# A two-layer hybrid decoder trunk on one core: the bytes at which the matmul operands start in SBUF are moved

## The chip, the cores and the metric

The program runs on one core of one Trainium2 chip. The metric is device time in microseconds (us) of one execution. The engines are named as in the profile: PE (TensorE matmul), PEld (TensorE weight load, which overlaps PE), DVE (VectorE), ACT (ScalarE), POOL (GpSimd), SP (SyncE, which here only issues DMAs). SBUF is the on-chip working memory of 128 partitions, PSUM the accumulators that the matmuls write. "Address" below always means the byte at which a buffer starts within each partition of SBUF.

## The reference, cut to what matters

```python
D_MODEL, SEQ, DEPTH = 2048, 256, 2            # one batch, float32 everywhere
def reference(x, ...):
    for l in range(DEPTH):
        h = rms_norm(x, norm_w[l])
        u = h @ w_in[l]                       # 2048 x 7692, cut into 12 parts
        y_conv = conformer_conv(...) * silu(c_gate)    # GLU, depthwise conv of 31, LayerNorm, 512x512 matmul
        y_gdn  = gated_deltanet(...)                   # 6 heads, chunked delta rule
        y_att  = dilated_attention(...) * silu(a_gate) # 12 heads, three strided windows
        x = x + concatenate([y_conv, y_gdn, y_att]) @ w_out[l]   # 2048 x 2048
    return rms_norm(x, final_norm_w)
```

The two large products, by `w_in` and `w_out`, are most of the arithmetic.

## The kernel before

**Precision by three products.** The matmuls of L448 and L457 take float32r operands. To keep float32 accuracy, every operand is held as a high part and a low part: the normalised activations in `HT[0]`, `HT[1]`, the branch outputs in `YT[0]`, `YT[1]`, and each block of weights, after its DMA into a `raw` buffer, as `whi` (ACT, L188) and `wlo = raw - whi` (DVE, L196). A product is then three matmuls: high by high, low by high, high by low.

**The two forms of a product.** `unit` (L448) makes the matmuls of one k-block (128 rows of the product's inner dimension). Where the result is wanted with channels on the partitions (`chan`), 128 columns of `whi` or `wlo` are loaded as stationary weights and 256 columns of `HT[..][:, k, :]` stream past: 18 or 24 matmuls for a k-block pair of a 384- or 512-wide block, each of 256 columns. Otherwise 128 columns of `HT` or `YT` are the stationary operand and the 384 (or 396, 512, 256) columns of `whi` or `wlo` stream. Every matmul has a weight load of 128 columns of its own, and the load for the next matmul runs while the present one streams. `last_unit` (L457) does the last block of the last layer, whose split weights are kept in `HT`: there 128 columns of `YT` are stationary and 256 columns of `HT` stream, 96 matmuls in all.

```python
if chan:
    o = acc[t // 2][:, (t % 2) * S:(t % 2 + 1) * S]
    terms = [(hi[:, a, s], A[0][:, k, :]), (hi[:, a, s], A[1][:, k, :]), (lo[:, a, s], A[0][:, k, :])]
else:
    o = acc[t][:, :n]
    terms = [(A[0][:, k, s], hi[:, a, :n]), (A[1][:, k, s], hi[:, a, :n]), (A[0][:, k, s], lo[:, a, :n])]
```

**The order of the work.** A small planner (`Plan`) runs generators as tasks against guessed costs and thereby writes one fixed order of instructions for each engine. The projections run back to back; between their matmuls stand the small float32 matmuls (`mms`, L229) and transposes (`trs`, L236) of the three branches. A layer takes its jobs in this order: scalars and gates, the delta-rule and convolution inputs (mostly `chan`), the attention inputs (not `chan`), the remaining gates (`chan`), then `w_out` in blocks of 384 and 512 (not `chan`). The weights come through 4 `raw`, 3 `whi` and 3 `wlo` buffers of 4 KB a partition, used in turn. The planner knows no addresses.

**Where buffers lie.** Tiles are placed in the order in which they are made, pool after pool: `cp` (constants and the operands `HT`, `YT`), `wp` (`raw`, `whi`, `wlo`), `sp` (work buffers `b768`, `b1024` and so on, all called `b` in the profile). The first tile of `cp` starts at byte 16,512, behind 16,384 bytes for DMA descriptors and four constants. A k-block of `HT` or `YT` is 1,024 bytes, a stationary slice of 128 columns 512 bytes, and a `whi` row of 384 columns 1,536 bytes, so within a form all operands stand at one and the same remainder of 512 bytes. (The 396-wide block of each layer is the exception: its second k-block stands 48 bytes further.)

Of the kernel before, what the change touches and what calls it, by code (L numbers as in the profile page):

```python
# [11 lines left out]
F32 = mybir.dt.float32  # L12
# [16 lines left out]
NT = S // 128  # L29
# [9 lines left out]
W_OUT_BLOCKS = [[(384 * i, 384) for i in range(4)] + e for e in ([(1536, 512)], [(1536, 256), (1792, 256)])]  # L39

P_CW, P_DW, P_DB, P_LW, P_LB, P_GN, P_AL, P_DT, PCOLS = 16, 88, 212, 216, 220, 224, 225, 231, 237


class Event:
# [128 lines left out]
def hybrid_trunk(ctx, tc, x, x_t, w_in, conf_pw_w, w_out, params, final_norm_w, rope, lnc, out):  # L173
    nc = tc.nc
    cp = ctx.enter_context(tc.tile_pool(name="consts", bufs=1))
    wp = ctx.enter_context(tc.tile_pool(name="weights", bufs=1))
# [18 lines left out]
    def tt(out_, a, b, op):  # L195
        return ("dve", 70 + _free(out_) / 0.96, lambda: nc.vector.tensor_tensor(out_, a, b, op=op))  # L196

    def ts(out_, a, s1, s2, op0, op1=None):
        extra = 60 if not isinstance(s1, (int, float)) else 0

        def emit():
            if op1 is None:
                nc.vector.tensor_scalar(out_, a, s1, None, op0=op0)  # L203
            else:
                nc.vector.tensor_scalar(out_, a, s1, s2, op0=op0, op1=op1)
        return ("dve", 70 + _free(out_) / 0.96 + extra, emit)
# [44 lines left out]
    def many(n, cols, name, dt=F32, pool=None):  # L251
        return Slots([(pool or sp).tile([128, cols], dt, name=f"{name}{i}", tag=f"{name}{i}") for i in range(n)])

    HT = [cp.tile([128, KB, S], F32R, name=f"HT{i}") for i in range(2)]
    YT = [cp.tile([128, KB, S], F32R, name=f"YT{i}") for i in range(2)]
    RAW = Slots([wp.tile([128, 1024], F32, name=f"raw{i}") for i in range(4)])
    WHI = Slots([wp.tile([128, 1024], F32R, name=f"whi{i}") for i in range(3)])
    WLO = Slots([wp.tile([128, 1024], F32R, name=f"wlo{i}") for i in range(3)])
    S768 = many(14, 768, "b768_")
    S1024 = many(3, 1024, "b1024_")  # L260
    S512 = many(2, 512, "b512_")
# [22 lines left out]
    upper = cp.tile([128, 128], F32, name="upper")  # L284
    lower = cp.tile([128, 128], F32, name="lower")
    lowr = cp.tile([128, 128], F32R, name="lowr")
    lncs = cp.tile([128, 384], F32, name="lncs")
    ropes = cp.tile([128, NT, 32], F32, name="ropes")
    pw_neg = cp.tile([128, HC], F32, name="pw_neg")
    PAR = [cp.tile([128, PCOLS], F32, name=f"par{l}") for l in range(DEPTH)]  # L290
    GNH = [cp.tile([128, 1], F32, name=f"gnh{l}") for l in range(DEPTH)]
# [7 lines left out]
           for l, p in enumerate([X_PIECES] + [PIECES] * (DEPTH - 1) + [LAST_PIECES])]  # L299
    RSTD = [cp.tile([128, NT], F32, name=f"rstd{l}") for l in range(DEPTH + 1)]  # L300
    sums = cp.tile([128, NT], F32, name="sums")
    HALF = [cp.tile([128, NT], F32, name=f"half{l}") for l in range(DEPTH)]
    ROW = [cp.tile([128, S], F32, name=f"row{l}") for l in range(DEPTH)]
    misc_ready = [Event() for _ in range(DEPTH)]
# [31 lines left out]
    def split(hi, lo, src, scale):  # L336

        yield act(hi, src, scale=scale)
        yield stt(lo, src, scale, hi.bitcast(F32), ALU.mult, ALU.subtract)
# [19 lines left out]
    def load_xt(k0, m):  # L359

        buf = yield ("get", S768)
        yield ("dma", 128 * m * S * 4 / 330.0, lambda: nc.sync.dma_start(  # L362
# [3 lines left out]
    def norm_xt(k0, m, buf):  # L366
        yield ("wait", misc_ready[0])
        for b in range(m):
            k = k0 + b
            yield from split(HT[0][:, k, :], HT[1][:, k, :], buf[:, b * S:(b + 1) * S], PAR[0][:, k:k + 1])  # L370
            yield ("set", h_ready[0][k])
        yield ("put", S768, [buf])

    def load_x(j):

        c0, n = X_PIECES[j]
        buf = yield ("get", S768)
        xs = buf[:, :NT * n].rearrange("p (t c) -> p t c", t=NT)
        yield ("dma", 128 * NT * n * 4 / 330.0, lambda: nc.sync.dma_start(
            xs, xf[:, c0:c0 + n].rearrange("(t p) c -> p t c", p=128)))  # L380
        plan.spawn(sums_x(j, xs, buf), 3)
        if j == len(X_PIECES) - 1:
            nc.sync.dma_start(lncs, lnc)
            nc.sync.dma_start(ropes, rope.rearrange("(t p) c -> p t c", p=128))

    def sums_x(j, xs, buf):
        yield from square_sums(0, j, [xs[:, t] for t in range(NT)], nsq0[j])
        yield ("put", S768, [buf])

    def load_weights(order):  # L390
        for i in order:
# [3 lines left out]
            if i in X_BEFORE:  # L395
                yield from load_x(X_BEFORE[i])
            raw = yield ("get", RAW)
            view = raw[:, :m * n].rearrange("p (a n) -> p a n", n=n)
# [8 lines left out]
    def split_weights(order):  # L407
        for i in order:
# [3 lines left out]
            if keep is None:  # L412
                hb = yield ("get", WHI)
                lb = yield ("get", WLO)
                hi, lo = (b[:, :m * n].rearrange("p (a n) -> p a n", n=n) for b in (hb, lb))
                w_ready[i][1] = (hi, lo, hb, lb)
            else:
                hi, lo = (b[:, keep:keep + m, :] for b in HT)
                w_ready[i][1] = (hi, lo, None, None)
# [9 lines left out]
    def split_lo(i, hi, lo, raw, view, e):  # L429
        yield ("wait", e)  # L430
        yield tt(lo, view, hi.bitcast(F32), ALU.subtract)
        yield ("put", RAW, [raw])
        yield ("set", w_ready[i][0])

    def unit(acc, hi, lo, a, n, A, k, first, last, chan):


        def emit():
            for t in range(n // 128 if chan else NT):
                s = slice(t * 128, (t + 1) * 128)  # L440
# [6 lines that stand above are left out]
                for i, (w, m) in enumerate(terms):  # L447
                    nc.tensor.matmul(o, w, m, start=first and i == 0 and not (chan and t % 2), stop=last and i == 2,  # L448
                                     skip_group_check=chan)
        return ("pe", 6 * (n / 2.4 + 2.5), emit)  # L450

    def last_unit(acc, t, k, n):

        def emit():
            s = slice(t * 128, (t + 1) * 128)
            for i, (w, m) in enumerate(((0, 0), (1, 0), (0, 1))):
                nc.tensor.matmul(acc[t][:, :n], YT[w][:, k, s], HT[m][:, k, :n], start=k == 0 and i == 0,  # L457
                                 stop=k == KB - 1 and i == 2)
        return ("pe", 3 * (n / 2.4 + 2.5), emit)

    def project(jobs):
# [15 lines left out]
        for (A, ready, w, c0, n, order, then, prio, before, chan), first in todo:  # L477
# [10 lines left out]
            for i, (k0, m) in enumerate(order):  # L488
                yield ("wait", w_ready[first + i][0])
                hi, lo, hb, lb = w_ready[first + i][1]  # L490
                for a in range(m):
                    k = k0 + a
                    yield ("wait", ready[k])
                    yield unit(acc, hi, lo, a, n, A, k, i + a == 0, i == len(order) - 1 and a == m - 1, chan)
                yield ("put", WHI, [hb])
                yield ("put", WLO, [lb])
            plan.spawn(then(acc), prio)
# [7 lines left out]
    def square_sums(l, j, xs, ev):  # L505
        for t in range(NT):
            yield act(JUNK[:, :_free(xs[t])], xs[t], AF.Square, accum=SSQ[l][:, t, j:j + 1])
        yield ("set", ev)
# [26 lines left out]
    def norm_128(l, k, ps, xs, done):  # L535
        yield trs(*((ps[:, t * 128:(t + 1) * 128], xs[t]) for t in range(NT)))
        yield ("wait", misc_ready[l])
        yield from split(HT[0][:, k, :], HT[1][:, k, :], ps, PAR[l][:, k:k + 1])
        yield ("set", h_ready[l][k])
        yield ("set", done)  # L540

    def finish_norm(l, evs, t0=0, t1=NT):
# [9 lines left out]
        if l == DEPTH:  # L552
            yield ("set", final_ready[t0])
            return
        yield ts(HALF[l], r, 0.125, None, ALU.mult)
        yield ("set", rstd_ready[l])
# [7 lines left out]
    def layer(l):  # L564
        par = PAR[l]
        cw, dw = par[:, P_CW:P_CW + 72], par[:, P_DW:P_DW + 4 * CW]
        rstd, half = RSTD[l], HALF[l]
        y_ready = [Event() for _ in range(KB)]
# [129 lines left out]
        def v3(t):  # L698

            return t.rearrange("p (a b) -> p a b", b=128)  # L700

        def scalars(acc):
            z = yield ("get", S768)
            gd["Z1"] = z.rearrange("p (t c) -> p t c", t=NT)
# [29 lines left out]
        def decay(b):  # L734
            t, i = divmod(b, 2)
            if i == 0:
                gd["EM"][t], gd["L%d" % t] = (v3(b_) for b_ in (yield ("get", S768, 2)))
                yield ("set", gd["E"][t])
# [490 lines left out]
        def inp(c0, n, then, prio, chan=False):  # L1229
            order = full if l or jobs else halved  # L1230
            jobs.append((HT, h_ready[l], win, c0, n, order, then, prio, None, chan))
        inp(GZ + 384, 396, scalars, 6)
# [98 lines left out]
```

## Time and profile before

| | |
|---|---|
| time, 3 runs | median 982.97 us (981.93 to 983.8) |
| the profiled execution's own time | 982.4 us |
| its span, first to last instruction | 980.7 us |
| PE busy | 968.4 us, 99% of the span, 7259 matmuls |
| PEld busy | 946.3 us, 96% |
| DVE busy | 749.3 us, 76% |
| ACT busy | 550.8 us, 56% |
| DMA | 179.01 MB, mean 183 GB/s |
| mean granted TensorE clock | 0.997 of full speed |

The matmuls' ends are modelled by the profiler, and one matmul's duration (some 280 ns for 256 columns) overlaps those of its neighbours; what a matmul costs the stream is the distance from its start to the start of the next. That distance is read here from the chain of work that ended last: where a piece of the chain is nothing but matmuls of one shape, its length divided by their number is the distance.

### The profile page before, as it was taken

What the parts mean: (1) busy time and instruction counts of PE and PEld (TensorE: products, weight loads), DVE (VectorE), ACT (ScalarE), POOL (GpSimd) and SP (SyncE); (2) the same over time, 40 slices, a digit from 0 to 9 for tenths busy, and PEclk for the clock granted to TensorE, in tenths of its full rate; (3) what the DMA queues carried; (4) which work ended last, traced back from release to release, by engine and by line L of the source; (5) the groups of instructions that cost most, each with busy time, mean ns of one, the idle gap of its engine ahead of it and who ended that gap; (6) DMA issues with size and microseconds to landing.
All of it is one profiled execution on the core that took longest, in us unless ns stands there. A gap on an engine that the chain in (4) does not pass through costs nothing.

```text
span 980.7 us, 19060 instructions
## 1 busy us (share of the span) xinstructions
PE 968.4 (99%) x7259; PEld 946.3 (96%) x7259; DVE 749.3 (76%) x1519; ACT 550.8 (56%) x1079; POOL 48.5 (5%) x70
## 2 busy tenths in 40 slices
PE   8999999999999999999999999999999999999996
PEld 7999999999999999999899999999899999999996
DVE  7687799999999666655558768999999976666672
ACT  7764355446685764554455633554466767544551
POOL 1002100200010000000000020002000100000000
PEclk9999999999999999999999999999999999999998
DMA  9765565644445535776655545556344556366672
GB/s 328 254 195 169 175 191 180 186 146 145 146 138 174 178 113 181 224 239 219 214 190 193 192 161 175 186 180 188 128 147 140 155 182 200 127 192 213 220 248 87
DMA packets 67037, 179.01 MB, mean 183 GB/s; under 512 B 8000, under 2 KB 12224, under 8 KB 66944
## 3 DMA queue, kind: packets, MB, share of 16 engines
q1 hardware_dynamic: 64880, 173.85, 54.7%
q0 software_dynamic: 1632, 3.02, 1.2%
q8 instruction: 57, 0.93, 0.4%
q10 hardware_dynamic: 432, 0.91, 0.3%
q14 instruction: 36, 0.29, 0.1%
HBM read 172.77 MB, written 4.98 MB: 181 GB/s over the span
## 4 chain that ended last, share of the span: by engine, by line
PE 97%; DVE 1%; DMA 1%; issue 1%; SPq 0%; ACT 0%; POOLq 0%; POOL 0%; DVEq 0%; ACTq 0%
PE acc L448 87%; PE mix L229 6%; PE mix L236 3%; DMA b<-in_x_t 1%; PE acc L457 1%; PE mix L747 0%; DVE wlo L196 0%; DVE b L193 0%; SPq L404 0%; SPq L362 0%; DVE inv L209 0%; ACT whi L188 0%; POOLq L1327 0%; POOL rstd L245 0%; DVE PTs L203 0%
## 5 line engine op out<-in xcount | busy, mean ns | idle before, releaser
L188 ACT ACTIVATE whi<-raw 128x768 fp32r<-128x768 f32 (+4 forms) x389 | 339.7, 873 | 361.4 <-PE acc L448 320.6
L196 DVE TENSOR_TENSOR wlo<-raw,whi 128x768 fp32r<-128x768 f32 (+4 forms) x389 | 385.5, 991 | 186.4 <-ACT whi L188 182.7
L448 PE MATMUL acc<-HT,whi 128*128 128x256 f32 x2304 | 411.0, 280 | 0.0
L448 PEld LDWEIGHTS acc<-HT,whi 128*128 128x128 f32 x2304 | 351.6, 188 | 1.5 <-issue 1.5
L448 PE MATMUL acc<-HT,wlo 128*128 128x256 f32 x1152 | 321.4, 279 | 0.0
L448 PE MATMUL acc<-whi,HT 128*128 128x384 f32 (+1 forms) x1024 | 271.1, 346 | 0.7 <-ACT whi L188 0.6
L448 PEld LDWEIGHTS acc<-HT,wlo 128*128 128x128 f32 x1152 | 216.0, 188 | 0.0
L448 PEld LDWEIGHTS acc<-whi,HT 128*128 128x128 f32 x1024 | 180.1, 189 | 3.3 <-ACT whi L188 1.4
L448 PE MATMUL acc<-wlo,HT 128*128 128x384 f32 (+1 forms) x512 | 172.9, 338 | 0.8 <-DVE wlo L196 0.8
L448 PE MATMUL acc<-whi,YT 128*128 128x384 f32 (+2 forms) x640 | 163.0, 338 | 0.0
L193 DVE SCALAR_TENSOR_TENSOR b<-b,par,b 128x255 f32<-128x255 f32 (+20 forms) x348 | 153.6, 465 | 0.3
L448 PEld LDWEIGHTS acc<-whi,YT 128*128 128x128 f32 x640 | 114.3, 187 | 2.8
L448 PE MATMUL acc<-wlo,YT 128*128 128x384 f32 (+2 forms) x320 | 107.9, 337 | 0.0
L448 PEld LDWEIGHTS acc<-wlo,HT 128*128 128x128 f32 x512 | 96.2, 188 | 1.8 <-DVE wlo L196 1.8
L448 PEld LDWEIGHTS acc<-wlo,YT 128*128 128x128 f32 x320 | 60.1, 188 | 1.5
L188 ACT ACTIVATE b<-mix 128x384 f32<-128x384 f32 (+3 forms) x96 | 39.6, 425 | 20.1 <-PE mix L229 12.6
L229 PE MATMUL mix<-b,b 128*128 128x128 f32 (+5 forms) x456 | 46.0, 285 | 0.0
L236 PE MATMUL mix<-ident,b 128*128 128x128 f32 x280 | 45.7, 274 | 0.0
L229 PEld LDWEIGHTS mix<-b,b 128*128 128x128 f32 (+3 forms) x456 | 36.2, 161 | 6.7 <-issue 2.2
L236 PEld LDWEIGHTS mix<-ident,b 128*128 128x128 f32 x280 | 34.2, 140 | 3.7 <-issue 1.3
L193 DVE SCALAR_TENSOR_TENSOR b<-b,b 128x256 f32<-128x256 f32 (+3 forms) x62 | 31.5, 511 | 2.6 <-ACT b L188 2.5
L188 ACT ACTIVATE b<-b,stat 128x128 f32<-128x128 f32 (+1 forms) x68 | 29.1, 442 | 6.0 <-DVE stat L203 5.9
(146 smaller groups left out, 613.2 us busy)
## 6 DMA issues: line engine op xcount, KB each, us to landing
raw<-in_w_in SPq DMA_DIRECT2D x240, 384.0 KB, 3.0
raw<-in_w_in SPq DMA_DIRECT2D x48, 512.0 KB, 3.6
raw<-in_w_out SPq DMA_DIRECT2D x64, 384.0 KB, 3.6
raw<-in_w_out SPq DMA_DIRECT2D x12, 512.0 KB, 4.1
raw<-in_w_in SPq DMA_DIRECT2D x15, 396.0 KB, 3.7
b<-in_x SPq DMA_DIRECT2D x10, 256.0 KB, 5.7
raw<-in_conf_pw_w SPq DMA_DIRECT2D x4, 512.0 KB, 3.2
raw<-in_w_out SPq DMA_DIRECT2D x8, 256.0 KB, 3.5
```

Source lines behind the costliest of these rows:

```text
L188: lambda: nc.scalar.activation(out_, in_, func, bias=bias, scale=scale, **kw))
L193: lambda: nc.vector.scalar_tensor_tensor(out_, a, s, b, op0=op0, op1=op1))
L196: return ("dve", 70 + _free(out_) / 0.96, lambda: nc.vector.tensor_tensor(out_, a, b, op=op))
L229: nc.tensor.matmul(o, a, b, start=f[0], stop=f[1])
L236: nc.tensor.transpose(o, a, ident)
L448: nc.tensor.matmul(o, w, m, start=first and i == 0 and not (chan and t % 2), stop=last and i == 2, skip_group_check=chan)
L457: nc.tensor.matmul(acc[t][:, :n], YT[w][:, k, s], HT[m][:, k, :n], start=k == 0 and i == 0, stop=k == KB - 1 and i == 2)
```

## The change

No instruction is added, removed or moved: on each of the five engines the operations stand in the same order, with the same operands and shapes. Only addresses change. `lncs` and `ropes` (1,536 and 256 bytes) are made first instead of later, a filler tile of 128 bytes follows them, one of 64 bytes stands further back in `cp`, one of 64 bytes between `raw` and `whi`, and one of 448 bytes behind `wlo`.

```diff
+PAD = (32, 16)
...
+    lncs = cp.tile([128, 384], F32, name="lncs")
+    ropes = cp.tile([128, NT, 32], F32, name="ropes")
+    cp.tile([128, PAD[0]], F32, name="pad0")
     HT = [cp.tile([128, KB, S], F32R, name=f"HT{i}") for i in range(2)]
     YT = [cp.tile([128, KB, S], F32R, name=f"YT{i}") for i in range(2)]
     RAW = Slots([wp.tile([128, 1024], F32, name=f"raw{i}") for i in range(4)])
+    wp.tile([128, 16], F32, name="gap0")
     WHI = Slots([wp.tile([128, 1024], F32R, name=f"whi{i}") for i in range(3)])
     WLO = Slots([wp.tile([128, 1024], F32R, name=f"wlo{i}") for i in range(3)])
+    wp.tile([128, 112], F32, name="gap1")
...
-    lncs = cp.tile([128, 384], F32, name="lncs")
-    ropes = cp.tile([128, NT, 32], F32, name="ropes")
...
     sums = cp.tile([128, NT], F32, name="sums")
+    cp.tile([128, PAD[1]], F32, name="pad1")
```

What this makes of the addresses in the built programs (remainders of 512 bytes; all were and are multiples of 64 bytes for the large buffers):

| buffer | first one at, before | after | mod 512 before | after |
|---|---|---|---|---|
| `HT0`, `HT1`, `YT0`, `YT1` | 16,512 | 18,432 | 128 | 0 |
| `ident` (of the transposes) | 91,264 | 93,184 | 128 | 0 |
| `raw0` to `raw3` | 100,160 | 100,352 | 320 | 0 |
| `whi0` to `whi2`, `wlo0` to `wlo2` | 116,544 | 116,800 | 320 | 64 |
| `b768`, `b1024`, other work buffers | 141,120 | 141,824 | 320 | 0 |

So the distance between the two operands of a matmul, modulo 512 bytes, becomes 64 instead of 192 for L448 (weights ahead of the activations), stays 0 for L457 (`YT` and `HT`), and becomes 0 instead of 192 for the transposes of work buffers. `HT` and `YT` are on multiples of 2 KB after the change.

## Rows read from the trace of the kernel before

**Rows 1.** The page: span, busy time by engine, granted clock, the chain that ended last.
```profile
span 980.7 us, 19060 instructions
PE 968.4 (99%) x7259; PEld 946.3 (96%) x7259; DVE 749.3 (76%) x1519; ACT 550.8 (56%) x1079; POOL 48.5 (5%) x70
...
PEclk9999999999999999999999999999999999999998
...
PE acc L448 87%; PE mix L229 6%; PE mix L236 3%; DMA b<-in_x_t 1%; PE acc L457 1%; PE mix L747 0%; DVE wlo L196 0%; DVE b L193 0%; SPq L404 0%; SPq L362 0%; DVE inv L209 0%; ACT whi L188 0%; POOLq L1327 0%; POOL rstd L245 0%; DVE PTs L203 0%
```

**Rows 2.** What PE waited for, whole span: engine, releaser, us, times, longest.
```profile
PE mix L311 <- POOL pw_neg L316: 1.6, 1, 1.6
PE acc L448 <- DVE wlo L196: 0.8, 2, 0.4
PE acc L448 <- ACT whi L188: 0.6, 1, 0.6
```

**Rows 3.** Groups of PE by shape, whole span: count, busy us, mean ns of one.
```profile
L448 PE MATMUL acc<-HT,whi 128*128 128x256 f32 x2304 | 411.0, 280 | 0.0
L448 PE MATMUL acc<-HT,wlo 128*128 128x256 f32 x1152 | 321.4, 279 | 0.0
...
L448 PE MATMUL acc<-whi,HT 128*128 128x384 f32 x896 | 236.7, 345 | 0.0
L448 PE MATMUL acc<-wlo,HT 128*128 128x384 f32 x448 | 150.6, 336 | 0.0
L448 PE MATMUL acc<-whi,YT 128*128 128x384 f32 x512 | 131.5, 338 | 0.0
L448 PE MATMUL acc<-wlo,YT 128*128 128x384 f32 x256 | 86.3, 337 | 0.0
L236 PE MATMUL mix<-ident,b 128*128 128x128 f32 x280 | 45.7, 274 | 0.0
```

**Rows 4.** The chain, layer 0, 256 columns: start us, us, engine, line, count.
```profile
93.23 2.01 PE mix L229 x18
95.24 41.49 PE acc L448 x366
136.72 0.22 PE mix L236 x2
136.94 6.13 PE acc L448 x54
143.08 0.22 PE mix L236 x2
143.30 10.61 PE acc L448 x90
```

**Rows 5.** The chain, layer 1: the same jobs as in rows 4, then a later gate.
```profile
575.78 44.53 PE acc L448 x378
620.31 0.22 PE mix L236 x2
620.53 6.36 PE acc L448 x54
...
834.97 8.36 PE acc L448 x72
```

**Rows 6.** The chain, layer 0, `w_out`, blocks of 384 columns.
```profile
416.15 0.66 PE mix L236 x6
416.81 16.97 PE acc L448 x96
433.78 0.65 PE mix L236 x6
434.43 16.65 PE acc L448 x96
```

**Rows 7.** The chain in layer 1's `w_out`, 884 to 946 us, 384 columns.
```profile
883.85 62.19 PE acc L448 x352
```

**Rows 8.** The chain near the end: L457, 256 columns.
```profile
960.87 5.77 PE acc L457 x48
```

**Rows 9.** PE groups of four stretches: 97:136, 577:619, 436:449 and 884:940 us.
```profile
L448 PE MATMUL acc<-HT,wlo 128*128 128x256 f32 x115 | 31.7, 276 | 0.0
...
L448 PE MATMUL acc<-HT,wlo 128*128 128x256 f32 x120 | 33.5, 279 | 0.0
...
L448 PE MATMUL acc<-wlo,YT 128*128 128x384 f32 x25 | 8.4, 335 | 0.0
...
L448 PE MATMUL acc<-wlo,YT 128*128 128x384 f32 x106 | 35.8, 338 | 0.0
```

**Rows 10.** Stretches: length, busy us of PE, PEld, DVE, ACT, POOL; clock, DMA.
```profile
95.00:142.00 47.00, 47.00 (x418) 47.00 (x416) 37.30 (x75) 20.48 (x29) 6.34 (x11) 1.00 0.57 178
142.00:181.00 39.00, 39.00 (x326) 39.00 (x325) 36.61 (x81) 21.57 (x46) 0.00 (x0) 1.00 0.57 181
181.00:328.00 147.00, 147.00 (x1068) 141.92 (x1068) 133.96 (x315) 90.26 (x199) 11.00 (x12) 1.00 0.50 157
575.00:662.00 87.00, 87.00 (x742) 87.00 (x742) 72.41 (x146) 41.68 (x75) 3.89 (x7) 1.00 0.55 178
882.00:950.00 68.00, 68.00 (x389) 68.00 (x388) 44.56 (x60) 35.85 (x54) 0.00 (x0) 1.00 0.72 228
960.90:968.60 7.70, 7.70 (x66) 7.70 (x66) 2.68 (x11) 1.53 (x6) 0.57 (x1) 1.00 0.00 0
```

## The prediction

> **What bounds the kernel now.** I read the page first: PE is busy for 99% of the span, the chain that ended last runs through L448 for 87% of it, and the clock is granted in full but for the last slice [rows 1]. The waits come next: PE waited for other engines for about 3 us in all, once for a constant at the start and otherwise under 1 us on each releaser [rows 2]. So nothing feeds PE too late; the time is the sum of the distances from one matmul's start to the next, and a change that moves no instruction can act only through those distances.
>
> The chain gives them. The same jobs, 256 columns a matmul, ran at 41.49 / 366 = 113.4 ns in layer 0 [rows 4] and at 44.53 / 378 = 117.8 ns in layer 1 [rows 5]. A piece further on in layer 0, after a pair of transposes, again has 10.61 / 90 = 117.9 ns. With 384 columns one block of `w_out` took 16.97 / 96 = 176.8 ns and the next 16.65 / 96 = 173.4 ns [rows 6]; in layer 1 the piece of 352 took 176.7 ns [rows 7]. L457 is the third rhythm: 256 columns, 5.77 / 48 = 120.2 ns [rows 8]. The clock is 1.00, the 2.4 GHz level, in all these stretches, and the DMA does not set the rhythm: it moved 0 GB/s beside L457, 178 beside 113.4 ns as beside 117.8, and 228 beside 176.7; nor does DVE, busy 79% beside 113.4 ns and 83% beside 117.8 [rows 10]. So there are fixed rhythms for one and the same matmul: fast (113.4, 173.4), slow (117.8, 176.7) and, where both operands lie at the same remainder of 512 bytes, slowest (120.2). A rhythm holds until PE is interrupted, as by the transposes in rows 4. The profiled durations carry it too: 276 ns goes with 113.4, 279 to 280 with 117.8, 335 with 173.4 and 338 with 176.7 [rows 9].
>
> At 2.4 GHz 256 columns are 106.7 ns and 384 are 160.0 ns. Something costs each matmul 7 to 17 ns beyond its columns. My reading is that the two streams that PE takes from SBUF, the moving columns and the next weights, get into each other's way where they come to the same part of a 512-byte period, and that the slow rhythm is the same pair of streams locked in a worse phase. L457 against L448 is the only pair in this trace that differs in the distance of its operands (0 against 192 bytes); that the distance is the cause is argued, not shown.
>
> **The change part by part.** No operation is added or removed, so the terms are counts times changes of a distance.
>
> First, L448 with 256 columns: 2,304 + 1,152 = 3,456 matmuls [rows 3]. Fast now are the pieces of 366 and 54 in layer 0 [rows 4] and the 72 at 835 us in layer 1 (8.36 / 72 = 116.1 ns, with a wait in front of it) [rows 5]: 492. The other 2,964 are slow. If all of them fall into the fast rhythm, 2,964 x (117.8 - 113.4) = 13.0 us come back.
>
> Second, L448 with 384 columns: 896 + 448 on `HT` and 512 + 256 on `YT` [rows 3]. The `wlo` groups, which hold almost no waits, tell the mixture: a mean of 336 ns on `HT` lies a third of the way from 335 to 338, a mean of 337 on `YT` two thirds [rows 3, 9]. So about 1,344 / 3 + 768 x 2 / 3 = 960 are slow; 960 x (176.7 - 173.4) = 3.2 us. The 96 matmuls of 512 and 192 of 396 columns I leave as they are.
>
> Third, what gets worse. The transposes' operands (`ident` and a work buffer) come to distance 0, from 192. Six transposes take 0.65 us, 108.3 ns each [rows 6]; small matmuls of L229 whose operands are both work buffers, at distance 0 already, take 2.01 / 18 = 111.7 ns [rows 4]. 280 transposes [rows 3] x 3.4 ns = 1.0 us lost. L457 keeps its distance of 0 and its 120 ns.
>
> Fourth, what hides elsewhere. The split on ACT and DVE and the DMAs into `raw` get new addresses too. If DVE's part became dearer by a few per cent it would not show as long as PE waits for it for under 1 us [rows 2]. A faster PE uses up some of that cover: in the tightest stretch, 142 to 181 us, DVE is busy 36.61 of 39 us, and the 286 matmuls there would give back about 1.3 us, so the stretch would shrink to 37.7 us with DVE still at 97%. From 181 to 328 us DVE is busy 133.96 of 147 us and about 1 us is to be gained [rows 10]. The cover holds; if it did not, these two stretches and their likes in layer 1 would withhold at most 4 to 5 us.
>
> Sum: 13.0 + 3.2 - 1.0 = 15.2 us. From the profiled execution's 982.4 us that gives 967.2; the median of the runs stands 0.6 us above that execution, so I predict 967.8, rounded to 968 us.
>
> Bounds, for the rhythm at a distance of 64 is in no row. From below: were nothing lost between the streams, a matmul of 256 columns would still wait for its own weight load, and loads of 128 columns follow each other at 108.3 ns in the transposes [rows 6]; 2,964 x 9.5 + 492 x 5.1 = 30.7 us. With 384 columns the limit is the columns, 160.0 ns: 960 x 16.7 + 1,152 x 13.4 = 31.5 us. Together 62 us less: 921 us. From above: all of L448 at L457's 120.2 ns, and 384 columns in proportion at 180.3 ns, is 2,964 x 2.4 + 492 x 6.8 + 960 x 3.6 + 1,152 x 6.9 = 21.9 us more, with the transposes 1,006 us. Of these I take neither end but the fast rhythm, since it is the nearest that the same matmuls were seen to hold without a break for 366 in a row.
>
> The Trainium skill speaks against any effect: "SBUF — State Buffer", section "Who interferes with whom", says that PE never waits on anyone for SBUF, and "TensorE: Matmul & The Clock Gate", section "Step-by-step: what each phase is for", that PE reads moving columns and weights through two independent ports, so that loading the next weights takes nothing from the running matmul. By that rule the sum would be 0 and the time 983 us. The three rhythms at one clock do not fit ports that never meet, though no row shows that the addresses are what sets them.
>
> **The rivals.** *No change, 983 us.* The rhythm is drawn anew whenever PE is interrupted, whatever the addresses. For it: the jobs of rows 4 and 5 stand at the same remainders of 512 bytes in both layers and still differ. Against it: L457, the one case at distance 0, shows a rhythm that L448 holds nowhere for long, and 256 columns fell into the slow rhythm in six cases of seven, which is no fair draw. The page's rule above gives this rival as well. Within it the transposes' 1.0 us may or may not show: 982 to 985 us.
>
> *Slower, 990 to 1,006 us.* 64 bytes is nearer to 0 than 192 is. If the cost falls with the distance, the change moves L448 toward L457: at the least the 492 + 1,152 fast ones become slow (492 x 4.4 + 1,152 x 3.3 = 6.0 us, with the transposes 990 us), at the most all run as L457 does (1,006 us). It decides once the mean of the 256-column matmuls passes today's (2,964 x 117.8 + 492 x 113.4) / 3,456 = 117.2 ns. For it: the only trend that the rows hold, 192 to 0, goes that way. Against it: 64 bytes may lie outside the part that a stream occupies, and at distance 192 both rhythms occur, so the phase counts besides the distance.
>
> *Much faster, 921 us.* The streams no longer meet at all. Against it: in neither form of L448, streaming `HT` or streaming the weights, was a piece faster than the fast rhythm. "TensorE: Matmul & The Clock Gate", section "Back-to-back issue gap", gives columns / 2.4 + 2.5 ns for one matmul, that is 109.2 and 162.5 ns; by this estimate the time would lie near 930 us. No row here reaches it.
>
> **How the numbers follow.** Forecast (the fast rhythm for most of L448, 960 to 977 us) 0.51; much faster 0.10; no change 0.17; slower 0.22. A measurement of this kernel can tell about 0.2%, 2 us, from no change; so faster 0.61, same 0.17, slower 0.22. The range, 943 to 992 us, leaves out most of "much faster" (0.08) and the worse half of "slower" (0.11); its width is that of the unknown rhythm at 64 bytes. The forecast's own range is 960 to 977 us.
>
> **What would show it.** In the changed kernel's groups the 256-column matmuls of L448 should have a mean duration of 276 ns, and the 384-column ones on `YT` 335; the counterpart of the piece at 575.78 us should take 113.4 ns a matmul. Transposes in sixes should take 0.67 us instead of 0.65. L457 should stay at 120. PE's waits on DVE should stay under 5 us. Wrong would be: both rhythms still mixed as before (no change), 283 ns in L448 (slower), or durations under 276 (much faster). If the rhythm is fast and the time is not, the new wait on `wlo` will be in PE's waits.

## The result, and the profile after

The changed kernel takes 972.93 us (median of 4 runs, 972.81 to 973.58) against 983.38 us (981.93 to 984.21) for the kernel before: a ratio of 0.9893, 95% interval 0.9881 to 0.9906. It is faster by 1.1%, inside the range of 943 to 992 us, and 5 us above the 968 us that were predicted. Lines of the source stand 3 or 7 further: L232 is L229, L239 is L236, L455 is L448, L464 is L457.

The page of the changed kernel, its span and busy times:

```profile
span 971.2 us, 19060 instructions
PE 958.6 (99%) x7259; PEld 937.3 (97%) x7259; DVE 748.1 (77%) x1519; ACT 550.8 (57%) x1079; POOL 48.6 (5%) x70
```

What PE waited for in it (us, times, longest):

```profile
PE acc L455 <- ACT whi L191: 1.1, 1, 1.1
PE acc L455 <- DVE wlo L199: 0.6, 2, 0.4
```

PE is still the whole story: 99% of a span that is 9.5 us shorter, and no new wait beside those of [rows 2]. DVE's 748 us fit into the shorter span without holding PE up.

PE's groups by shape in the changed kernel, as in [rows 3]:

```profile
L455 PE MATMUL acc<-HT,whi 128*128 128x256 f32 x2304 | 404.7, 280 | 0.0
L455 PE MATMUL acc<-HT,wlo 128*128 128x256 f32 x1152 | 320.5, 278 | 0.0
...
L455 PE MATMUL acc<-whi,YT 128*128 128x384 f32 x512 | 130.6, 336 | 0.0
L455 PE MATMUL acc<-wlo,YT 128*128 128x384 f32 x256 | 86.0, 336 | 0.0
L239 PE MATMUL mix<-ident,b 128*128 128x128 f32 x280 | 45.8, 274 | 0.0
...
L455 PE MATMUL acc<-whi,YT 128*128 128x512 f32 x64 | 19.9, 393 | 0.0
...
L455 PE MATMUL acc<-YT,whi 128*128 128x256 f32 x64 | 11.3, 279 | 0.0
```

The mean of the 1,152 went from 279 to 278 ns, where 276 had been expected; that of the 384 columns on `YT` went from 338 and 337 to 336, where 335 had been expected. (Of the 2,304 the mean hides the change, since some of them follow an interruption; their busy time went from 411.0 to 404.7 us.)

The chain of the changed kernel in layer 0, the counterpart of [rows 4]:

```profile
93.72 41.50 PE acc L455 x366
135.23 0.22 PE mix L239 x2
135.44 6.36 PE acc L455 x54
141.81 0.22 PE mix L239 x2
142.03 10.23 PE acc L455 x90
```

and in layer 1, the counterpart of [rows 5]:

```profile
569.62 44.52 PE acc L455 x378
614.15 0.22 PE mix L239 x2
614.37 6.16 PE acc L455 x54
620.52 0.22 PE mix L239 x2
620.74 10.23 PE acc L455 x90
```

Some pieces became fast, one became slow, and one stayed slow. The piece of 90 in layer 0 went from 117.9 to 10.23 / 90 = 113.7 ns, the piece of 54 behind the long one from 113.5 to 117.8, the long piece of layer 1 is as slow as ever at 44.52 / 378 = 117.8 ns, and the two pieces behind it are fast now (6.16 / 54 = 114.1 and 113.7 ns). Both rhythms are those of before; more pieces stand in the fast one.

The chain through layer 0's `w_out` (384 columns), then layer 1's, then L464, the counterparts of [rows 6 to 8]:

```profile
412.19 0.65 PE mix L239 x6
412.84 16.64 PE acc L455 x96
429.49 0.66 PE mix L239 x6
430.14 16.64 PE acc L455 x96
...
879.92 60.15 PE acc L455 x347
...
951.38 5.76 PE acc L464 x48
```

With 384 columns all these pieces are fast: they take 16.64 / 96 = 173.3 ns in both blocks, and 60.15 / 347 = 173.3 ns in layer 1 where it was 176.7. L464 kept its distance of 0 and its 120.0 ns. Six transposes still take 0.65 or 0.66 us.

Where the 9.5 us came from can be added up. The trace gives every matmul's start; the distance from one start to the next, summed over all matmuls of L448 and L457 whose successor follows without an interruption (counted as such up to 30 ns beyond the number of columns divided by 2.4 GHz):

| columns | matmuls | before, us | after, us | difference |
|---|---|---|---|---|
| 256 | 3,689 | 432.5 | 425.8 | -6.7 |
| 384 | 2,000 | 349.7 | 346.7 | -3.0 |
| 396 | 176 | 31.8 | 32.1 | +0.3 |
| 512 | 95 | 22.2 | 21.8 | -0.4 |

Together -9.7 us; the span shrank by 9.5. Of the 3,496 `chan` matmuls with a `chan` successor, 498 stood 113 or 114 ns from the next one before, and 2,005 do now.

### The profile page after: what moved, and what is told of

It reads as the page before. It is cut to its first block, busy times and chain, and to the rows that moved or that the text cites. A ratio compares the mean times of both kernels' runs of the same rounds, so it can differ in the third digit from the quotient of the medians.

```text
span 971.2 us, 19060 instructions
## 1 busy us (share of the span) xinstructions
PE 958.6 (99%) x7259; PEld 937.3 (97%) x7259; DVE 748.1 (77%) x1519; ACT 550.8 (57%) x1079; POOL 48.6 (5%) x70
## 4 chain that ended last, share of the span: by engine, by line
PE 97%; DVE 1%; DMA 1%; issue 1%; SPq 0%; ACT 0%; POOLq 0%; POOL 0%; DVEq 0%; ACTq 0%
PE acc L455 87%; PE mix L232 6%; PE mix L239 3%; DMA b<-in_x_t 1%; PE acc L464 1%; PE mix L754 0%; DVE wlo L199 0%; DVE b L196 0%; SPq L411 0%; SPq L369 0%; DVE inv L212 0%; ACT whi L191 0%; POOLq L1334 0%; POOL rstd L248 0%; DVE PTs L206 0%
## 5 line engine op out<-in xcount | busy, mean ns | idle before, releaser
L455 PE MATMUL acc<-HT,whi 128*128 128x256 f32 x2304 | 404.7, 280 | 0.0
L455 PEld LDWEIGHTS acc<-HT,whi 128*128 128x128 f32 x2304 | 350.4, 189 | 1.5 <-issue 1.5
L455 PE MATMUL acc<-HT,wlo 128*128 128x256 f32 x1152 | 320.5, 278 | 0.0
L455 PE MATMUL acc<-whi,HT 128*128 128x384 f32 (+1 forms) x1024 | 270.8, 346 | 1.1 <-ACT whi L191 1.1
L455 PEld LDWEIGHTS acc<-HT,wlo 128*128 128x128 f32 x1152 | 216.3, 188 | 0.0
L455 PEld LDWEIGHTS acc<-whi,HT 128*128 128x128 f32 x1024 | 180.2, 189 | 3.4 <-ACT whi L191 1.5
L455 PE MATMUL acc<-wlo,HT 128*128 128x384 f32 (+1 forms) x512 | 173.1, 338 | 0.6 <-DVE wlo L199 0.6
L455 PE MATMUL acc<-whi,YT 128*128 128x384 f32 (+2 forms) x640 | 161.8, 336 | 0.0
L455 PEld LDWEIGHTS acc<-whi,YT 128*128 128x128 f32 x640 | 113.9, 188 | 2.4
L455 PE MATMUL acc<-wlo,YT 128*128 128x384 f32 (+2 forms) x320 | 107.5, 336 | 0.0
L455 PEld LDWEIGHTS acc<-wlo,HT 128*128 128x128 f32 x512 | 96.3, 188 | 1.6 <-DVE wlo L199 1.6
L455 PEld LDWEIGHTS acc<-wlo,YT 128*128 128x128 f32 x320 | 60.1, 188 | 1.4
L232 PE MATMUL mix<-b,b 128*128 128x128 f32 (+5 forms) x456 | 45.9, 285 | 0.0
L239 PE MATMUL mix<-ident,b 128*128 128x128 f32 x280 | 45.8, 274 | 0.0
L232 PEld LDWEIGHTS mix<-b,b 128*128 128x128 f32 (+3 forms) x456 | 36.2, 161 | 6.6 <-issue 2.2
L239 PEld LDWEIGHTS mix<-ident,b 128*128 128x128 f32 x280 | 34.1, 141 | 3.8 <-issue 1.3
```

The source lines that it names most:

```text
L232: nc.tensor.matmul(o, a, b, start=f[0], stop=f[1])
L239: nc.tensor.transpose(o, a, ident)
```

## The experiments

The theory to be tested is the prediction's: the distance between a matmul's two operands in SBUF sets the rhythms it can fall into. The rivals: the absolute place of `HT` and `YT` did it; or each interruption draws a rhythm, whatever the addresses; or the place of the weights' parts did it, whatever they meet. All kernels below are the changed kernel with other fillers; no instruction moves in any. "Distance" is the address of the weights' parts minus that of `HT`, modulo 512, unless said otherwise.

**Distance 0.**

```diff
-    wp.tile([128, 16], F32, name="gap0")
-    wp.tile([128, 112], F32, name="gap1")
+    wp.tile([128, 128], F32, name="gap1")
```

> The changed kernel with the weights' parts moved back by 64 bytes, so that they stand on multiples of 512 as HT and YT do: distance 0 between the operands of every large matmul. Theory 'distance' (the remainder of 512 bytes between the two streams sets the rhythm): 256 columns run at L457's 120 ns, 384 at about 180 ns; time about 1,003 us (995 to 1,010). Theory 'place' (it is HT and YT on multiples of 2 KB that helped): 973 us as the changed kernel. Theory 'redrawn' (the rhythm is drawn at each interruption, whatever the addresses): between 968 and 985 us with both rhythms mixed.

Measured: 989.78 us, 1.0067 of the kernel before (1.0052 to 1.0082). "Place" and "redrawn" fall: `HT` and `YT` are where the changed kernel has them, and it is 17 us slower. The counterpart of the long piece of layer 1, in its chain:

```profile
580.46 0.67 PE mix L232 x6
581.13 45.36 PE acc L454 x378
```

45.36 / 378 = 120.0 ns, L457's rhythm, as foreseen, and so in nearly all pieces of 256 columns. The time missed the 995 to 1,010 us because the other half of the expectation was wrong: 384 columns do not scale from 120 to 180 ns. At distance 0 they kept the fast rhythm (one group of `chan`, then two of `w_out`):

```profile
L454 PE MATMUL acc<-HT,wlo 128*128 128x256 f32 x1152 | 325.8, 283 | 0.0
...
L454 PE MATMUL acc<-whi,YT 128*128 128x384 f32 x512 | 130.2, 335 | 0.0
...
L454 PE MATMUL acc<-wlo,YT 128*128 128x512 f32 x32 | 12.5, 390 | 0.0
```

**Distance 192, the one of the kernel before.** `gap0` has 48 columns, `gap1` 80.

> The changed kernel with the weights' parts 192 bytes past multiples of 512 instead of 64, HT and YT still on multiples of 2 KB: the distance of the kernel before at the places of the changed one. 'Distance': the rhythms of the kernel before, some 980 to 985 us, with 384 columns partly at 176.7 ns. 'Place': 973 us. 'Redrawn': anything from 968 to 985 us.

Measured: 984.32 us, 1.0010 of the kernel before (1.0000 to 1.0019). Moving `HT` and `YT` to multiples of 2 KB is worth nothing by itself, nor is anything else in the change but the distance of the weights. One thing is not as before, though the distance of L448 is the same: the long piece of layer 0, at 113.4 ns in [rows 4], has the slow rhythm here, 43.11 / 366 = 117.8 ns:

```profile
95.53 43.11 PE acc L455 x366
```

So at one distance the other addresses have a say in which of its two rhythms a piece takes.

**Everything shifted by 128 bytes, distances as changed.**

```diff
-PAD = (32, 16)
+PAD = (64, 16)
```

> The changed kernel with every buffer from HT on 128 bytes further: HT and YT 128 past multiples of 2 KB as in the kernel before, all distances as in the changed one. 'Distance': 973 us (971 to 975), 384 columns all at 173.4 ns. 'Place': back to about 983 us. 'Redrawn': 968 to 985 us.

Measured: 972.53 us, 0.9893 (0.9878 to 0.9908). Its groups are those of the changed kernel:

```profile
L455 PE MATMUL acc<-HT,wlo 128*128 128x256 f32 x1152 | 320.5, 278 | 0.0
...
L455 PE MATMUL acc<-wlo,YT 128*128 128x384 f32 x256 | 86.0, 336 | 0.0
```

With the two runs before, this settles it between the theories: distance, not place. The place of the weights' parts falls too: `whi0` starts at byte 116,928 both here and in the run at 192, and only `HT`, `YT` and the other buffers stand 128 bytes apart; the times are 972.53 and 984.32 us.

**The changed kernel again.** No edit.

> The changed kernel once more, for a second profile of the same program. If the slow rhythm of a piece is drawn anew at each interruption, then the pieces of 256 columns that run at 117.8 ns are others than in the first profile, and their share moves by several points. If addresses and the order of instructions settle it, the same pieces are slow. Time 973 us either way if the mean over many pieces holds.

Measured: 973.25 us, 0.9897 (0.9883 to 0.9912). Its chain in layer 0:

```profile
93.07 41.50 PE acc L455 x366
134.57 0.22 PE mix L239 x2
134.79 6.36 PE acc L455 x54
141.15 0.22 PE mix L239 x2
141.37 10.23 PE acc L455 x90
```

Piece by piece the rhythms of the first profile: fast, slow, fast. Of the 3,689 uninterrupted matmuls of 256 columns, 3,603 were in the same rhythm in both profiles; nearly all others belong to three short pieces of 23 to 32 matmuls. So a rhythm is settled where the stream restarts, but for the most part it is not drawn by chance: the same program at the same addresses repeats it. What in the restart decides was not tried.

**Distances 32, 128, 256, 448** (`gap0` of 8, 32, 64, 112 columns, `gap1` the rest of 128).

> The changed kernel with the weights' parts 32 bytes past multiples of 512. Theory 'smooth' (the cost falls gradually with the distance from 0): between distance 0 and 64, so 256 columns at 117 to 119 ns and a time of 978 to 986 us. Theory 'piece' (what counts is whether the two streams stand in the same 64-byte piece): as distance 0, 256 columns at 120 ns, about 990 us.

Measured: 985.64 us, 1.0032 (1.0021 to 1.0043). As "smooth" had it, 256 columns at 118.3 ns on average; "piece" falls.

> The weights' parts 128 bytes past multiples of 512, half way between the changed kernel's 64 and the 192 of the kernel before. 'Smooth' between two measured points: 256 columns at 116 to 117 ns, 384 at 173.4 to 175 ns, 975 to 983 us. If the phase in which the streams lock after an interruption decides, it can lie outside of these: the fast rhythm throughout would be about 966 us, the slow one throughout about 989 us.

Measured: 990.49 us, 1.0083 (1.0066 to 1.0101), as slow as 0, 160 and 256 within the intervals. Interpolation between 64 and 192 fails by 7.5 us. The expectation's other branch, the slow rhythm throughout at about 989 us, is 1.5 us off.

> The weights' parts 256 bytes past multiples of 512: as far from the activations as a period of 512 allows. Theory 'far is good' (cost falls with distance either way round): not slower than distance 192, 984 us or less. Theory 'just ahead' (the weights' stream should stand a little ahead of the moving one, which runs twice as fast past it): at least as slow as 192, 984 to 990 us.

Measured: 991.02 us, 1.0080 (1.0065 to 1.0095). "Far is good" falls. "Just ahead" is about 1 us off its range, but the groups say something simpler:

```profile
L455 PE MATMUL acc<-HT,wlo 128*128 128x256 f32 x1152 | 325.8, 283 | 0.0
...
L455 PE MATMUL acc<-whi,YT 128*128 128x384 f32 x512 | 130.2, 335 | 0.0
...
L455 PE MATMUL acc<-wlo,YT 128*128 128x512 f32 x32 | 12.5, 390 | 0.0
```

To the last digit these are the rows at distance 0. So 0 and 256 are the same distance, while 64 and 192 are not: the period is 256 bytes, not the 512 of the prediction.

> The weights' parts 448 bytes past multiples of 512, that is 64 bytes behind the activations modulo 512 where the changed kernel has them 64 ahead. Theory 'symmetric' (only the distance either way round counts): 973 us, the 256-column matmuls in the same mixture. Theory 'just ahead': 256 columns slow (117.8 ns or more), 980 to 992 us.

Measured: 984.52 us, 1.0021 (1.0012 to 1.0030). "Symmetric" falls. The time and the 117.8 ns are as "just ahead" had them, for a reason that it did not have: 448 is 192 modulo 256, where the time was 984.32. The two kernels' `wlo` groups, 192 first:

```profile
L455 PE MATMUL acc<-HT,wlo 128*128 128x256 f32 x1152 | 321.8, 279 | 0.0
```

```profile
L455 PE MATMUL acc<-HT,wlo 128*128 128x256 f32 x1152 | 321.8, 279 | 0.0
```

**Distances 96 and 224** (`gap0` of 24 and 56 columns).

> The weights' parts 96 bytes past multiples of 512. So far the remainder of 256 bytes tells all: 0 and 256 alike, 192 and 448 alike; at 32, 64 and 128 the 256-column matmuls took 118.3, 115.4 and 118.8 ns on average. Theory 'valley at 64': 96 lies between 64 and 128, 116 to 118 ns, 975 to 988 us. Theory 'each 32 bytes has its own locking': no interpolation holds, anything between 965 and 992 us.

Measured: 989.69 us, 1.0064 (1.0047 to 1.0081); 256 columns at 118.1 ns, 0.1 above what "valley at 64" gave. The time lies above that theory's range as well, since 384 columns, whose own distance (defined below the runs) is 160, took 176.6 ns:

```profile
L455 PE MATMUL acc<-wlo,YT 128*128 128x384 f32 x256 | 86.7, 339 | 0.0
```

> The weights' parts 224 bytes past multiples of 512, 32 behind the activations modulo 256. Theory 'symmetric about 0': as distance 32, 985 us. Theory 'just ahead is best, just behind is not' (64 gave 973 us and its mirror image 448 gave 984.5): 985 to 992 us, with the 256-column matmuls at 118 to 120 ns.

Measured: 979.10 us, 0.9956 (0.9941 to 0.9971), with 256 columns at 116.8 ns. Both theories miss: 32 behind is better than 32 ahead.

**`YT` alone 64 bytes further.** What stands behind `YT` moves by 256 bytes, one whole period.

```diff
+    cp.tile([128, 16], F32, name="gap2")
     YT = [cp.tile([128, KB, S], F32R, name=f"YT{i}") for i in range(2)]
+    cp.tile([128, 48], F32, name="gap3")
```

> The changed kernel with YT alone 64 bytes further; HT, the weights' parts and all else stand at the same remainder of 256 bytes as before. Theory 'pair' (the distance between the two operands of one matmul decides): only products with YT change. L457 goes from distance 0 to 64 and from 120 ns to between 113 and 118; w_out goes to distance 0, where 512 columns took 227.4 ns and 384 173.4 ns; the 256-column matmuls of the pointwise product go to 120 ns; the attention inputs and the chan products of HT keep their rhythms. Together within 1 us of the changed kernel. Theory 'place of the weights' (it is where the weights' parts stand that decides, whatever they meet): L457 stays at 120 ns and w_out at 173.4 and 229 ns.

Measured: 971.64 us (971.13 to 973.46), 0.9882 (0.9866 to 0.9899). Its groups that read `YT`, and one that doesn't (L457 here is L448 of the kernel before, L466 is its L457):

```profile
L457 PE MATMUL acc<-wlo,HT 128*128 128x384 f32 x448 | 150.6, 336 | 0.0
L457 PE MATMUL acc<-whi,YT 128*128 128x384 f32 x512 | 130.1, 335 | 0.0
...
L457 PE MATMUL acc<-whi,YT 128*128 128x512 f32 x64 | 19.8, 391 | 0.0
L457 PE MATMUL acc<-YT,whi 128*128 128x256 f32 x64 | 11.8, 285 | 0.0
...
L466 PE MATMUL acc<-HT,YT 128*128 128x256 f32 x96 | 11.1, 276 | 0.0
```

and the last product in the chain:

```profile
952.47 5.47 PE acc L466 x48
```

Each pair with `YT` did what its own distance says, and "place of the weights" falls once more: the last product, at 64 instead of 0, fell from 120.0 to 5.47 / 48 = 114.0 ns; the 512 columns of `w_out`, now at 0, took the 391 ns of the run at distance 0 instead of 393; the pointwise product, now at 0, rose from 279 to 285 ns; the attention inputs stayed. One part of the expectation failed: the `chan` products of `HT`, whose distance did not change, did not all keep their rhythms. In layer 1's remaining gates a piece of 287 went from slow to fast. Thirty us of it, first in the changed kernel, 30.15 / 256 = 117.8 ns, then here, 30.15 / 266 = 113.3 ns:

```profile
839.94 30.15 PE acc L455 x256
```

```profile
841.90 30.15 PE acc L457 x266
```

That alone is 287 x 4.5 ns = 1.3 us, as much as the two medians differ. It is the fastest of all the kernels, but the changed kernel's interval covers it: a gain over it is not shown by the time.

**Distance 160** (`gap0` of 40 columns).

> The weights' parts 160 bytes past multiples of 512, the last of the eight multiples of 32 below 256. With the pair theory a product tells its rhythm by weights minus moving operand, modulo 256: in the run at 96 the few 256-column matmuls of w_out stood at 160 and took 120.0 ns. So the 256-column products of HT should take 120 ns here, that is 16 us more than in the changed kernel; 384 columns stand at 96, which no run has had: 173.4 to 176.7 ns. Time 987 to 996 us. If only the place of the weights counted, any time between 965 and 992 us.

Measured: 990.61 us, 1.0079 (1.0062 to 1.0096). The 256 columns came at 119.9 ns, as 96 products of another pair had foretold:

```profile
L455 PE MATMUL acc<-HT,wlo 128*128 128x256 f32 x1152 | 325.5, 283 | 0.0
```

The whole of it, by the distance of each pair (stationary minus moving operand, modulo 256), in ns from start to start, means over uninterrupted matmuls. The 256-column ones are the `chan` products of `HT`; the others are L448's products with streaming weights, whose distance is the negative of the kernel's. That the sign goes by the role and not by the buffer is seen in the run at 192: there the 256-column products of `w_out`, weights streaming and so at 64, were fast, 113.4 ns, beside 117.8 of `chan` at 192:

```profile
L455 PE MATMUL acc<-whi,YT 128*128 128x256 f32 x64 | 10.9, 276 | 0.0
```

In the kernel before the same products had the slow rhythm, 117.8 ns. The means:

| distance of the pair | 256 columns | 384 columns | 512 columns |
|---|---|---|---|
| 0 | 119.8 | 174.1 | 227.4 |
| 32 | 118.3 | 173.8 | 233.3 |
| 64 | 115.3 | 174.9 | 233.3 |
| 96 | 118.1 | 173.7 | 234.2 |
| 128 | 118.8 | 176.0 | 232.4 |
| 160 | 119.9 | 176.6 | 233.4 |
| 192 | 117.8 | 173.4 | 229.1 |
| 224 | 116.8 | 174.4 | 233.3 |

Each mean is of one run; other addresses shift it a little, as with 256 columns at 192 (117.2 ns in the kernel before) and at 64 (114.9 with `YT` moved). The changed kernel has its 256 columns at 64, the best of the eight, and its 384 and 512 columns at 192, the best and the second best. The kernel before had them at 192 and 64: the change swaps the two.

## Why the prediction was right, and where its sizes were off

*The bound.* Right: PE's stream of matmuls is the time, and only distances from start to start changed. Their differences add up to 9.7 us, where the span shrank by 9.5; the other 0.2 us lies outside of the uninterrupted matmuls.

*The rhythms depend on the operands' distance.* Right, and now shown: the runs at 0, 192 and the shift by 128 separate distance from place, and the one with `YT` alone shows that the pairs whose distance changed went by it. That the two streams obstruct each other inside SBUF remains the reading; the runs show that the distance decides and with what period, not what happens there. The period was wrong: 256 bytes and not 512. Nor does the picture of two streams that come to the same part of the period fit what was measured: at 128 and 160, away from 0, 256 columns take 118.8 and 119.9 ns, nearly the 119.8 of distance 0.

*That 64 is a good distance.* Luck. The prediction had no row for 64 and no reason for it over another distance. Of the seven distances other than that of the kernel before, five made the kernel slower and two made it faster, 64 by 1.1% and 224 by 0.4%. The prediction also gave both forms of L448 one distance; by the pair's own sign 384 columns came to 192, which happens to be their best.

*First term, 13.0 us from 256 columns.* This is the step that was mis-sized: 6.7 us. I let all 2,964 slow matmuls become fast; about half of them did (113 or 114 ns for 2,005 instead of 498). The fast rhythm is available at distance 64, but the restart after an interruption still puts many pieces into the slow one. The 378 of layer 1 are among them, at 117.8 ns, where the prediction had named 113.4 as its sign. The 492 that were taken as fast at 192 were no property of that distance either: at the same distance and other addresses the 366 were slow.

*Second term, 3.2 us from 384 columns.* Right: 3.0 us, with means of 173.3 to 173.4 ns on `HT` and on `YT`.

*Third term, 1.0 us lost on the transposes.* Wrong: next to nothing. Sixes of them take 0.65 to 0.66 us at distance 0 and 0.65 to 0.66 at 192, and the group's busy time is 45.8 us where it was 45.7, so distance 0 does not cost the transposes the 3.4 ns; why the matmuls of L229 in [rows 4] take 111.7 ns is not shown.

*Fourth term, the cover.* Right: PE's waits for the split weights, from DVE and ACT, are 0.6 and 1.1 us.

*512 and 396 columns, left alone.* They moved by -0.4 and +0.3 us. The 396-wide block's second k-block stands 48 bytes further, at another distance.

*The rivals.* "No change" had the right observation, that an interruption sets the rhythm, and the wrong conclusion. The Trainium skill, "SBUF — State Buffer", section "Who interferes with whom", says that PE never waits on anyone. Taken as the prediction took it, all these kernels would need the same time; they span 971.6 to 991.0 us by addresses alone, so here the measurement decides against that reading. "Slower" assumed that nearness to 0 is bad. For 256 columns 0 is indeed nearly the worst, but the cost does not fall steadily away from it: 64 is the best and 160 as bad as 0. "Much faster" did not occur, here or at any distance: no piece of 256 columns went below 113 ns a matmul, and no mean of 384 columns below 173.

## What to carry to other kernels

Where PE is busy throughout, divide pieces of the chain by their number of matmuls; if one shape comes in two or three fixed spacings at a full clock, the operands' addresses are worth a trial, which costs a filler tile and moves no instruction. Vary the distance between moving and stationary operand in steps of 32 bytes over 256 bytes and judge each shape by its own spacing, since here 256 and 384 columns were best at different distances. Change one buffer at a time, and don't expect the mean of two neighbours in between. A gain of 1 or 2 us can also come from a piece that took its other rhythm, so look at the pieces before giving it to a distance.

## What the runs showed of the hardware that was not expected

- The spacing of float32r matmuls depends on the distance between their operands modulo 256 bytes: distances 0 and 256, and 192 and 448, gave the same group means of 256, 384 and 512 columns to the nanosecond, and the kernels from 0 to 224 differ by up to 18 us in 973.
- At one distance there can be two rhythms (113.3 and 117.8 ns at 64), held for hundreds of matmuls and settled at the restart; the same program repeats them: 3,603 of 3,689 matmuls. Addresses other than the pair's own change which one a piece takes (366 matmuls at 113.4 or 117.8 ns at distance 192, 287 at 117.8 or 113.3 ns at 64).
- No distance brought a shape down to its number of columns divided by the 2.4 GHz that were granted: the best means of the table are 115.3, 173.4 and 227.4 ns for 256, 384 and 512 columns, against 106.7, 160.0 and 213.3 ns.
